# A relative-bias table built in the first stage, with its row copies made from DRAM to DRAM in four pieces on SP's queue

## Chip, core and metric

The kernel runs on one core of one Trainium2 chip. The metric is device time in microseconds; before the change it is 1724.96 us, the median of three runs (1724.55 to 1725.47). The profile is of one further execution.

## What is computed

A transformer of three layers on 512 tokens of width 1024, in float32. The first block is a mixer (a pooling branch beside sparse attention), a cross attention to 256 memory tokens and a SwiGLU network; two hybrid layers of windowed attention and a state space model follow. The change touches the sparse attention alone. Of the reference:

```python
bias = rel_bias_table[_t5_bucket(q_pos[None, :, None] - sel)]
logits = logits + jnp.moveaxis(bias, -1, 1).astype(jnp.float32)
logits = jnp.where(valid[:, None], logits, -jnp.inf)
p = jax.nn.softmax(logits, axis=-1).astype(vg.dtype)
return jnp.einsum('bhtk,btkd->bhtd', p, vg)
```

Each of 8 heads adds to its logits a bias that depends only on the distance from query to key, looked up by bucket in a table of 32 rows. A query attends to the 128 keys with the highest index scores.

## The kernel before

All products are float32 split into two parts: a weight tile of [128, 1024] is loaded raw (`wraw`, three buffers, SP's queue), ScalarE copies its upper part (`whi`, L106), VectorE (DVE) subtracts to get the lower part (`wlo`, L109), and TensorE (PE) runs upper times upper (L148), upper times lower (L149) and lower times upper (L152). A "unit" is 128 output columns: 24 products of 512 tokens.

The order on PE, ScalarE, DVE and Pool (GpSimd) is set by a scheduler when the program is built; each engine then runs its list strictly in order. SP's list stands as the code issues it. A DMA issue that must wait for something holds its engine's queue, and so all that is behind it.

The stages that the change touches are the first (`mem_kv`) and the mixer (`mixer`):

- `mem_kv` multiplies the memory's keys (L646, four units) and values (L671), and meanwhile norms the tokens by halves: squares on ScalarE (L165, L168), sums on DVE (L169), a product with ones on PE that sums over partitions (L175), logarithm, exponential and a Newton step (L188 to L202), then for each of 8 tiles a DVE product (L216), a ScalarE copy (L130) and a DVE subtraction (L131) into the pairs `h`.
- `mixer` first runs three units by token halves, which need `h`. Then come four pool units with window sums and index scores between them, the key and value units, eight query units with the top-128 masks between them (`topk_mask`, DVE, L393 to L407), eight gates (a unit of 24 products, a tanh at L180) each with a product of the pool branch (12 products), and the eight heads. A head is twelve logits products (L523) into two PSUM banks (384 keys of query block 2 in one, 128 and 256 of blocks 0 and 1 in the other, then 512 of block 3 in the first again), a Pool add of bias tile and mask (L528), the softmax on DVE and ScalarE (L415 to L419), transposes (L541), one unit of the other gate between, and the values (L557 to L559).

`bias_tables` stands in the code between the masks and the gates. It loads the table and a one-hot matrix in two halves of 320 columns (L349), multiplies them on PE into a vector of 640 biases by distance for each head (L351, in `pstr`), copies the result to SBUF with DVE (L353, into `G`), and stores it 128 times per head into the DRAM scratch `ts`, [8, 128, 640], from ScalarE's queue (L354). `toeplitz` then loads a head's tile of 128 x 512 from `ts` (L360, ScalarE's queue) with a row step of 639, so that each row is shifted by one column.

Of the kernel before, what the change touches and what calls it, by code (L numbers as in the profile page):

```python
# [13 lines left out]
P = 128  # L14
# [9 lines left out]
# column blocks of the packed per-feature vectors  # L24
# [21 lines left out]
# units of an output projection that run by column halves  # L46
# [3 lines left out]
class Unit:  # L50
    """Weights of an output unit in [128, 512] tiles."""
# [10 lines left out]
class Kern:  # L62
    # [128, 512] four-byte tiles by role; the roles change with the phase
# [14 lines left out]
    # ---------------------------------------------------------------- helpers  # L78
# [20 lines left out]
    def weights(self, src, n=1024):  # L99
        """Load [128, n] raw weights; return them split as hi + lo."""  # L100
        nc = self.nc
        raw = self.wp.tile([P, 1024], F32, tag="wraw", bufs=3, name=self.nm("wraw"))
        nc.sync.dma_start(raw[:, :n], src)
        hi = self.wp.tile([P, 1024], F32R, tag="whi", bufs=3, name=self.nm("whi"))
        lo = self.wp.tile([P, 1024], F32R, tag="wlo", bufs=3, name=self.nm("wlo"))
        nc.scalar.copy(hi[:, :n], raw[:, :n])  # L106
        for o in range(0, n, S):
            c = slice(o, min(o + S, n))
            nc.vector.tensor_tensor(lo[:, c], raw[:, c], hi[:, c].bitcast(F32), ALU.subtract)  # L109
        return hi, lo  # L110

    def held(self, src, tag, n=1024):
        """as weights, in tiles of the activations"""
        nc = self.nc
        raw = self.wp.tile([P, 1024], F32, tag="wraw", bufs=3, name=self.nm("wraw"))
        nc.sync.dma_start(raw[:, :n], src)
        his, los = [], []
        for o in range(0, n, S):
            w = min(S, n - o)
            hi, lo = self.r(tag), self.r(tag)  # L120
            self.split(raw[:, o : o + w], hi[:, :w], lo[:, :w])
            his.append(hi)
            los.append(lo)
        return Unit(his), Unit(los)

    def split(self, src, hi, lo, scale=None):
        """hi + lo = src * scale, both float32r."""
# [13 lines left out]
    def mm3(self, out, w, xs, m=P, start=True, stop=True, woff=0):  # L141
        """out[m, N] += sum_k w_k^T x_k with w = (hi, lo) units and xs = list of (hi, lo)."""
# [28 lines left out]
    def rstd(self, rs, acc, eps, scale=1.0):  # L171
        """acc: per-partition sums of squares; rs = (scale * sum / 1024 + eps)^-0.5 on all partitions."""
        nc = self.nc
        pt = self.ps("tr")[:, : acc.shape[1]]
        nc.tensor.matmul(pt, self.ones, acc, start=True, stop=True)  # L175
        self.inv_sqrt(rs, pt, acc, eps, scale)
# [5 lines left out]
    def inv_sqrt(self, rs, src, u, eps=None, scale=1.0):  # L182
        """u = scale * src + eps, rs = u^-0.5: exp(-ln(u) / 2) and a Newton step; without eps src is u;
        the table with both functions is loaded behind the last square"""
# [19 lines left out]
    def pre_norm(self, gname, h):  # L204
        """returns a function that norms x's columns c into the pairs h"""
# [19 lines left out]
    def pre_scale(self, gname, h, rows=False):  # L225
        """x * g into the pairs h; the norm's token factor, for the products, into the tile returned, a column of it
        per token or, by rows, a row of it per token and a column per block"""
# [22 lines left out]
    def pump(self, n=99):  # L250
        """emit n pieces of the pending tail"""
# [4 lines left out]
    def tail(self, load, mm, use, chain, n, hold=False):  # L256
        """Units 0..7 of an output projection, the last n by column halves: the first half's chain runs under the
        second half's units, the second's under the next phase's first units."""
# [22 lines left out]
    def post_norm(self, gname, eps, otag, src, each, end=None, late=4, pool=(1, 3, 5, 7)):  # L281
        """x + rms_norm(o) * g for x given by src(k, columns): use(j, columns, o) takes o's units, chain(columns)
        has each(k, columns, t) get the sum, end(columns) end a half; DVE adds the squares of the units from late on,
        Pool has the products of the units in pool"""
# [24 lines left out]
    # ---------------------------------------------------------------- constants  # L309
# [32 lines left out]
    def bias_tables(self):  # L342
        """v[h, 511 - dist] = table[bucket(dist), h] in DRAM, a copy per row of the Toeplitz tiles of the T5 bias."""
        nc, a = self.nc, self.a
        tab = self.load("table", [32, 8])
        self.tv = self.dp.tile([8, P, 640], F32, tag="ts", name="ts")
        for c in (0, 320):
# [6 lines left out]
            nc.scalar.dma_start(self.tv[:, :, c : c + 320], v.unsqueeze(1).broadcast_to([8, P, 320]))  # L354

    def toeplitz(self, h):
        """T[p, m] = bias of head h at distance p - m + 384"""
# [5 lines left out]
    # ---------------------------------------------------------------- layer 1: mixer  # L363
# [21 lines left out]
    def topk_mask(self, score):  # L385
        """additive mask: 0 where a key is among the row's first 128, else NEG"""
# [23 lines left out]
    def softmax_rows(self, pt, pr):  # L410
        """pr = softmax(pt + pr) over the rows' columns"""
# [9 lines left out]
    def mixer(self):  # L421
# [4 lines left out]
        # indexer keys and weights  # L426
        # the first units by column halves: the norm of the second runs under them
# [20 lines left out]
        # pool mixer, the index scores in between  # L448
# [13 lines left out]
        for g in range(4):  # L462
# [15 lines left out]
            pooled.append(self.pair(mean, "R"))  # L478
            if g < 3:
# [3 lines left out]
        # shared key and value  # L483
# [15 lines left out]
        self.bias_tables()  # L499
        # gates; the pool branch  # L500
# [10 lines left out]
        # attention, the other gate's projection between the heads  # L511
# [21 lines left out]
        def transposed(prs):  # L533
            """P^T in two parts, for key block kt the query blocks from kt on"""
# [27 lines left out]
        # a head's logits go with the transposes and values of the head before, the other gate's projection in between  # L562
# [13 lines left out]
        # merge  # L576
# [7 lines left out]
        # twice the mixer's output: its norm takes four times the epsilon  # L584
# [12 lines left out]
    # ---------------------------------------------------------------- layer 1: memory  # L597
    def mem_kv(self):
        """keys and values of the memory; the norm's token factor is applied to the products"""
# [39 lines left out]
        for j in range(4):  # L639
# [5 lines left out]
            for k in range(KD):  # L645
                nc.tensor.matmul(pt, wk[j][:, k * P : k * P + P], mg[k], start=k == 0, stop=k == 7)  # L646
        self.h = self.pairs("G")
# [37 lines left out]
    def memory(self):  # L685
        """the tokens' halves one step apart: the first's attention with the second's queries, the second's with the
        first's output projection"""
# [15 lines left out]
        def logits(hd, c):  # L703
            """the probabilities of a half's two query blocks"""
# [81 lines left out]
    # ---------------------------------------------------------------- layer 1: ffn  # L786
    def ffn(self):
# [18 lines left out]
        # the first units by halves  # L806
# [35 lines left out]
    # ---------------------------------------------------------------- layer 2  # L842
# [10 lines left out]
    def hybrid(self, L):  # L853
# [3 lines left out]
        # dt = softplus(dt_raw + dt_bias), a_cs = cumsum(dt * a) within the chunks  # L857
# [3 lines left out]
        # halved convolution weights: conv / 2 feeds silu(x) = (1 + tanh(x / 2)) * (x / 2)  # L861
# [4 lines left out]
        def conv_part(y, j, c, pt, before=None):  # L866
            """y = (conv + bias) / 2 on columns c; before: the products of the columns before c"""
# [22 lines left out]
        # the rows 0..15 of dt's units take the weights' upper parts, the rows 32..47 the lower ones  # L890
# [6 lines left out]
        # the first units by halves  # L897
# [23 lines left out]
        # log1p(e) = ln(u) + (e - (u - 1)) / u with u = 1 + e rounded  # L921
# [15 lines left out]
        # token-major dt and a_cs: [128, chunk, head]  # L937
# [17 lines left out]
        # masked cb^T [s, l] for each group and chunk  # L955
# [10 lines left out]
        # token-major B  # L966
# [16 lines left out]
        def tokens(g):  # L983
            """token-major x * dt of group g, and the states at the chunks' ends"""
# [29 lines left out]
        def decay(j):  # L1014
            """masked cb^T * exp(a_cs[l] - a_cs[s]) of heads 2j, 2j + 1, and exp(a_cs[l])"""
# [17 lines left out]
        def heads(j, ws, ee):  # L1033
            """y of heads 2j, 2j + 1 in place of their xs"""
# [26 lines left out]
        # gate: twice y * silu(z), so the norm takes four times the epsilon  # L1061
# [21 lines left out]
        # sliding window attention: a head's products stack its queries' two parts along the rows, [hi | lo] for  # L1083
        # the even heads and [lo | hi] for the odd ones, and repeat its keys
# [29 lines left out]
        def scores(t, q):  # L1114
            """the probabilities of head t by query block: keys of the block before and its own"""
# [35 lines left out]
        def transposed(prs):  # L1151
            """P^T in two parts: for key block kb the query blocks kb, kb + 1"""
# [16 lines left out]
        def values(j, pts):  # L1169
            """the two heads of a pair share the array, each with half of its columns"""  # L1170
# [17 lines left out]
        # a head's scores go with the transposes of the head before, a unit of products in between  # L1188
# [23 lines left out]
        # out projection, deepnorm residual, layer norm  # L1212
# [80 lines left out]
# ------------------------------------------------------------------ host layout  # L1293
def _units(w):
    """[K, M] -> [M/128, 128, K]: unit u holds for partition p the 128 columns of each K tile."""
# [5 lines left out]
def _rows(w, n):  # L1301
    """[K, M] -> [128, K/128 * M] chunks of n K-tiles each."""
# [33 lines left out]
def layout(inp):  # L1336
# [21 lines left out]
    # attention heads of layer 2, in pairs: an even kv group's head with the next group's  # L1358
# [42 lines left out]
```

## Time and profile before

| | us |
|---|---|
| median of three runs | 1724.96 |
| span of the profiled execution, first to last instruction | 1719.3 |
| PE busy in the span | 1632.6 (95%) |
| DVE busy | 1146.6 (67%) |
| ScalarE busy | 849.0 (49%) |
| Pool busy | 249.6 (15%) |

The profile gives no time of its own for the profiled execution beyond its span; the median stands 5.7 us above the span, which is what lies around the first and last instruction. In the profile a line number names the code line, `out<-in` the tiles by their names, and an idle time is put down to the event that came last before the instruction began. A float32 product on PE that isn't split leaves two records. PE's clock is given as the share granted by the throttle. Waits of an engine other than PE cost time only where PE in turn waits for that engine.

### The profile page before, as it was taken

To read this page: it belongs to the slowest core of one execution; us is meant where nothing else is said; L and a number is where in the kernel's file an instruction comes from. 1 tells how busy PE (TensorE), PEld (TensorE's weight loads), DVE (VectorE), ACT (ScalarE), POOL (GpSimd) and SP (SyncE) were. 2 spreads that over 40 slices of the span, in tenths; PEclk is the share of its full clock that TensorE was granted. 3 is DMA by queue.
4 is the path that set the end of the run, shared out by engine and by line. 5 is a ranking of instruction groups with operands and counts; after the bars stand their busy time and mean duration, and the time that the engine had idled before them with its cause. 6 is when DMAs were issued, how large, how long until landed. Compare 5 with 4: busy or idle time off the path is not lost.

```text
span 1719.3 us, 24715 instructions
## 1 busy us (share of the span) xinstructions
PE 1632.6 (95%) x9078; PEld 1378.1 (80%) x9078; DVE 1146.6 (67%) x2495; ACT 849.0 (49%) x1664; POOL 249.6 (15%) x301
## 2 busy tenths in 40 slices
PE   8999919999898999999999999999999999999996
PEld 6788707888887888888998778787898777888786
DVE  7779517754878555552479876876479986876547
ACT  4532105534566333322366567666256567666424
POOL 2000012201321000000000023122121012312122
PEclk9999959999899999999999999999999999999998
DMA  7322432224224332223562312211253321221133
GB/s 249 126 80 68 101 72 93 72 81 152 87 66 144 98 98 98 93 92 99 149 209 74 121 52 74 74 62 62 91 175 118 114 71 62 74 74 62 62 100 121
DMA packets 59818, 170.70 MB, mean 99 GB/s; under 512 B 6737, under 2 KB 17937, under 8 KB 59697
## 3 DMA queue, kind: packets, MB, share of 16 engines
q1 hardware_dynamic: 49280, 156.79, 28.3%
q10 hardware_dynamic: 10416, 12.34, 3.0%
q8 instruction: 71, 1.16, 0.3%
q14 instruction: 51, 0.41, 0.1%
HBM read 160.18 MB, written 8.91 MB: 98 GB/s over the span
## 4 chain that ended last, share of the span: by engine, by line
PE 79%; DVE 10%; ACT 3%; another core or an unknown queue 3%; DMA 2%; issue 2%; POOL 1%; ACTq 1%; SPq 0%; DVEq 0%; POOLq 0%
PE psmm L152 21%; PE psmm L149 21%; PE psmm L148 21%; DVE wlo L109 2%; PE pstr L1162 1%; PE psmm L1177 1%; PE pstr L1041 1%; DMA wraw<-w_in 1%; PE psmm L646 1%; PE pslg L1133 1%; PE pstr L1047 1%; PE pslg L1134 1%; DVE ht L873 1%; DVE G L299 1%
## 5 line engine op out<-in xcount | busy, mean ns | idle before, releaser
L148 PE MATMUL psmm<-G,whi 128*128 128x512 f32 (+2 forms) x1420 | 525.2, 378 | 3.1 <-ACT whi L106 2.5
L149 PE MATMUL psmm<-G,whi 128*128 128x512 f32 (+2 forms) x1420 | 520.3, 374 | 2.3 <-DVE G L236 2.1
L109 DVE TENSOR_TENSOR wlo<-wraw,whi 128x512 fp32r<-128x512 f32 x541 | 374.4, 713 | 187.5 <-ACT whi L106 166.1
L106 ACT CAST whi<-wraw 128x1024 fp32r<-128x1024 f32 (+3 forms) x275 | 280.9, 1023 | 372.3 <-PE psmm L149 255.8
L152 PE MATMUL psmm<-G,wlo 128*128 128x512 f32 (+2 forms) x1420 | 328.8, 372 | 0.0
L148 PEld LDWEIGHTS psmm<-G,whi 128*128 128x128 f32 (+1 forms) x1420 | 266.7, 189 | 51.0 <-ACT whi L106 4.6
L149 PEld LDWEIGHTS psmm<-G,whi 128*128 128x128 f32 (+1 forms) x1420 | 267.2, 189 | 49.4 <-DVE G L236 3.4
L152 PEld LDWEIGHTS psmm<-G,wlo 128*128 128x128 f32 (+1 forms) x1420 | 251.2, 188 | 46.9 <-issue 1.0
L148 PE MATMUL psmm<-R,whi 128*128 128x256 f32 (+1 forms) x780 | 236.1, 325 | 2.9 <-ACT whi L106 2.3
L149 PE MATMUL psmm<-R,whi 128*128 128x256 f32 (+1 forms) x780 | 236.3, 325 | 1.9 <-DVE R L236 1.9
L148 PEld LDWEIGHTS psmm<-R,whi 128*128 128x128 f32 x780 | 149.1, 191 | 15.3 <-ACT whi L106 2.5
L149 PEld LDWEIGHTS psmm<-R,whi 128*128 128x128 f32 x780 | 149.4, 192 | 14.3 <-DVE R L236 2.7
L152 PE MATMUL psmm<-R,wlo 128*128 128x256 f32 (+1 forms) x780 | 146.9, 327 | 0.0
L152 PEld LDWEIGHTS psmm<-R,wlo 128*128 128x128 f32 x780 | 120.6, 193 | 11.8
L169 POOL TENSOR_TENSOR acc<-acc,sq 128x256 f32<-128x256 f32 (+1 forms) x58 | 61.3, 1061 | 444.4 <-ACT sq L168 439.3
L1143 ACT ACTIVATE w<-w,st 128x256 f32<-128x256 f32 (+1 forms) x128 | 60.1, 471 | 39.0 <-DVE st L1141 38.8
L1148 POOL TENSOR_SCALAR w<-w,st 128x256 f32<-128x256 f32 x64 | 40.5, 643 | 139.9 <-DVE st L1146 122.2
L873 DVE SCALAR_TENSOR_TENSOR ht<-psmm,cwh,ht 128x255 f32<-128x255 f32 (+5 forms) x96 | 57.6, 608 | 2.6 <-ACT ht L871 2.2
L523 PE MATMUL pslg<-G,R 128*128 128x384 f32 (+3 forms) x96 | 20.3, 349 | 40.4 <-DVE st L415 39.9
L528 POOL TENSOR_TENSOR G<-G,G 128x384 f32<-128x384 f32 (+2 forms) x24 | 25.4, 1070 | 211.9 <-DMA G<-ts 160.6
L802 DVE TENSOR_TENSOR sq<-psmm,G 128x512 f32<-128x512 f32 (+1 forms) x24 | 15.5, 646 | 59.0 <-PE psmm L152 58.9
L168 ACT ACTIVATE sq<-G 128x256 f32<-128x256 f32 (+1 forms) x76 | 35.2, 464 | 39.2 <-DVE G L1232 28.3
(322 smaller groups left out, 2331.3 us busy)
## 6 DMA issues: line engine op xcount, KB each, us to landing
wraw<-w_in SPq DMA_DIRECT2D x120, 512.0 KB, 3.4
wraw<-w_out SPq DMA_DIRECT2D x56, 512.0 KB, 3.8
wraw<-w_down SPq DMA_DIRECT2D x24, 512.0 KB, 3.5
wraw<-w_gate SPq DMA_DIRECT2D x22, 512.0 KB, 3.5
wraw<-w_up SPq DMA_DIRECT2D x22, 512.0 KB, 3.4
wraw<-w_down SPq DMA_DIRECT2D x12, 384.0 KB, 3.4
wraw<-w_proj_attn SPq DMA_DIRECT2D x8, 512.0 KB, 3.3
ts<-G ACTq DMA_DIRECT2D x2, 1280.0 KB
```

The lines of the kernel that those rows point to most:

```text
L106: nc.scalar.copy(hi[:, :n], raw[:, :n])
L109: nc.vector.tensor_tensor(lo[:, c], raw[:, c], hi[:, c].bitcast(F32), ALU.subtract)
L148: nc.tensor.matmul(out, whi[:, c], xh, start=start and k == 0, stop=False)
L149: nc.tensor.matmul(out, whi[:, c], xl, start=False, stop=False)
L152: nc.tensor.matmul(out, wlo[:, c], xh, start=False, stop=stop and k == n - 1)
L168: self.last_sq = nc.scalar.activation(t, src, AF.Square)
L169: (eng or nc.gpsimd).tensor_tensor(acc, acc, t, ALU.add)
L523: nc.tensor.matmul(pt, l[:, q], r[:, :N], start=n == 0, stop=n == 2)
L528: nc.gpsimd.tensor_tensor(pr, tb[:, 384 - P * i :], self.cmask if i == 0 else masks[i], ALU.add)
L873: nc.vector.scalar_tensor_tensor(z[:, s:], pt[:, : n - s], cw(3 - s), z[:, s:], ALU.mult, ALU.add)
L1143: nc.scalar.activation(prs[b], prs[b], AF.Exp, bias=nm[:, b : b + 1], accum_out=sm[:, b : b + 1])
L1148: (nc.gpsimd if b % 2 else nc.vector).tensor_scalar(prs[b], prs[b], rc[:, b : b + 1], 1.0, ALU.mult, ALU.mult)
```

## The change

The vector is now made in the first stage: `bias_tables` is called in `mem_kv` between the memory keys' products and the token norm. It stores the vector once, as `t1`, [8, 640], in DRAM. A new function `bias_rows` copies it to 32 of the 128 rows of all heads in `ts`, from DRAM to DRAM, on SP's queue; it is called once behind each of the four pool units.

```diff
@@ bias_tables
         tab = self.load("table", [32, 8])
+        self.v1 = self.dp.tile([8, 640], F32, tag="t1", name="t1")
         self.tv = self.dp.tile([8, P, 640], F32, tag="ts", name="ts")
...
             nc.vector.tensor_copy(v, pt[:8, :320])
-            nc.scalar.dma_start(self.tv[:, :, c : c + 320], v.unsqueeze(1).broadcast_to([8, P, 320]))
+            nc.scalar.dma_start(self.v1[:, c : c + 320], v)
+
+    def bias_rows(self, i):
+
+        rows = slice(32 * i, 32 * i + 32)
+        dst = self.tv[:, rows, :].rearrange("h p c -> p h c")
+        self.nc.sync.dma_start(dst, self.v1[:, :].unsqueeze(0).broadcast_to([32, 8, 640]))
@@ mixer, in the loop over the pool units
             pooled.append(self.pair(mean, "R"))
+            self.bias_rows(g)
             if g < 3:
@@ mixer, between the masks and the gates
-        self.bias_tables()
@@ mem_kv, behind the memory keys
                 nc.tensor.matmul(pt, wk[j][:, k * P : k * P + P], mg[k], start=k == 0, stop=k == 7)
+        self.bias_tables()
         self.h = self.pairs("G")
```

(Comments were blanked as well; from `bias_tables` on, line numbers after the change are 5 to 8 higher.)

The scheduler places the moved work anew. On PE in the first stage, the rows before, where `psmm_185` and `psmm_202` are the third and fourth unit of memory keys and the `pstr` rows are sums of the norms (`acc_227` that of the tokens' first half, `acc_88` that of the memory):

```order
L646 MATMUL psmm_185<-R_162,wraw_118 128x256
L175 MATMUL pstr_251<-acc_227,ones 128x256
L175 MATMUL pstr_292<-acc_88,ones 128x256
L655 MATMUL pstr_302<-ones,acc_88 128x1 x2
L646 MATMUL psmm_202<-R_128,wraw_194 128x256
...
L646 MATMUL psmm_202<-R_162,wraw_194 128x256
L671 MATMUL pslg_313<-wraw_315,R_128 128x512
L671 MATMUL pslg_314<-wraw_315,R_128 128x512
L671 MATMUL pslg_313<-wraw_315,R_132 128x512
L671 MATMUL pslg_314<-wraw_315,R_132 128x512
```

The same place after the change, where the rows with `table` are the two products with the one-hot and `acc_245` is the tokens' sum:

```order
L653 MATMUL psmm_185<-R_162,wraw_118 128x256
L352 MATMUL pstr_217<-G_215,table 8x320
L653 MATMUL psmm_202<-R_128,wraw_194 128x256
...
L653 MATMUL psmm_202<-R_162,wraw_194 128x256
L352 MATMUL pstr_224<-G_222,table 8x320
L175 MATMUL pstr_269<-acc_245,ones 128x256
L679 MATMUL pslg_331<-wraw_333,R_128 128x512
L175 MATMUL pstr_310<-acc_88,ones 128x256
L679 MATMUL pslg_332<-wraw_333,R_128 128x512
L663 MATMUL pstr_320<-ones,acc_88 128x1 x2
```

The sums of the norms moved behind the fourth key unit and both table products. Further down, the sum of the tokens' second half moved from behind the 9th to behind the 14th of the 16 value products.

On SP's queue at the pool units, before (`wraw` rows: the weights of the pool product, of the four pool units and of the key):

```order
L103 DMA wraw_629<-pool_w 128x512
L103 DMA wraw_639<-w_in 128x1024
L103 DMA wraw_714<-w_in 128x1024
L103 DMA wraw_802<-w_in 128x1024
L103 DMA wraw_893<-w_in 128x1024
L103 DMA wraw_957<-w_in 128x1024
```

And after:

```order
L103 DMA wraw_647<-pool_w 128x512
L103 DMA wraw_657<-w_in 128x1024
L361 DMA ts<-t_213 32x8x640
L103 DMA wraw_733<-w_in 128x1024
L361 DMA ts<-t_213 32x8x640
L103 DMA wraw_822<-w_in 128x1024
L361 DMA ts<-t_213 32x8x640
L103 DMA wraw_914<-w_in 128x1024
L361 DMA ts<-t_213 32x8x640
L103 DMA wraw_979<-w_in 128x1024
```

Each row copy stands between the weights of one unit and those of the next.

On ScalarE at the last gates, before (`sq` rows are the tanh of gates, `whi` rows casts of weights, `G<-ts` the loads of the first two heads' bias tiles):

```order
L349 DMA G_1515<-onehot 32x320
L354 DMA ts<-G_1512 1024x1x320
L354 DMA ts<-G_1519 1024x1x320
L180 ACTIVATE sq_1829<-psmm_1804 128x512
L180 ACTIVATE sq_1884<-psmm_1859 128x512
L106 CAST whi_1888<-wraw_1886 128x512
L106 CAST whi_1909<-wraw_1907 128x1024
L106 CAST whi_1943<-wraw_1941 128x512
L360 DMA G_1962<-ts 128x512
L106 CAST whi_2013<-wraw_2011 128x1024
L360 DMA G_2045<-ts 128x512
```

And after, from the tanh of the fifth gate on:

```order
L180 ACTIVATE sq_1779<-psmm_1754 128x512
L367 DMA G_1967<-ts 128x512
L106 CAST whi_1859<-wraw_1857 128x1024
L367 DMA G_2050<-ts 128x512
L106 CAST whi_1893<-wraw_1891 128x512
L180 ACTIVATE sq_1834<-psmm_1809 128x512
L106 CAST whi_1914<-wraw_1912 128x1024
L106 CAST whi_1948<-wraw_1946 128x512
L180 ACTIVATE sq_1889<-psmm_1864 128x512
```

The stores are gone from the queue, and the loads of the bias tiles moved ahead of the casts for the last gates. On PE the first head's first nine logits moved from between the seventh gate and its pool product to behind the last pool product, directly ahead of the other three; from the first head's end on, PE's order is unchanged. Pool's order is unchanged throughout.

## The prediction

> **What bounds the kernel now.** I read the chain of work that ended last first, because it names what the end depends on. Outside one place it is TensorE work. That place, in order of time (start, length, what):
>
> ```profile
> 193.42 8.54 ACTq L354
> 203.15 1.97 ACT whi L106 x3
> 205.12 44.38 another core or an unknown queue
> 249.57 2.60 DMA G<-ts
> ```
>
> The chain goes from the issue of the second table store (L354, on ScalarE's queue) through 44 us in which no engine acts to the load of the first head's bias tile. Next the busy time by stage around it (stretch, length, busy us of PE, PEld, DVE, ACT, POOL, then granted clock, DMA share, GB/s):
>
> ```profile
> 180.00:200.00 20.00, 20.00 (x86) 15.21 (x85) 12.69 (x35) 2.27 (x3) 0.00 (x0) 1.00 0.39 97
> 200.00:216.50 16.50, 14.23 (x58) 11.28 (x57) 3.28 (x5) 3.05 (x5) 0.00 (x0) 0.90 0.59 96
> 216.50:254.00 37.50, 0.07 (x2) 0.05 (x1) 0.67 (x3) 1.04 (x1) 1.70 (x3) 0.53 0.42 76
> 254.00:276.00 22.00, 19.51 (x74) 16.01 (x75) 16.86 (x51) 11.13 (x26) 5.95 (x6) 0.79 0.33 108
> 276.00:296.00 20.00, 19.84 (x110) 16.79 (x109) 14.79 (x52) 10.94 (x28) 7.55 (x8) 1.00 0.26 79
> ```
>
> From 216.5 to 254 all five engines stand still, and on both sides of it the granted clock is 0.90 and 0.79, so some work there runs slowly too. The waits of 185 to 290 us (who waits for whom: total, times, longest) say why:
>
> ```profile
> POOL G L528 <- DMA G<-ts: 160.6, 1, 160.6
> DVE G L415 <- POOL G L528: 47.2, 2, 46.8
> ACT whi L106 <- DMA ts<-G: 44.9, 1, 44.9
> PE pslg L523 <- DVE st L415: 39.9, 2, 37.4
> PE psmm L148 <- ACT whi L106: 2.3, 1, 2.3
> ```
>
> PE waits for the first softmax, DVE there for Pool's bias plus mask, Pool for the bias tile. The tile's load stands on ScalarE's queue waiting for the stores, and a weight cast stands 44.9 us behind it. The queues of 190 to 250 us (packets, MB, share of 16 engines; KB each, us to landing) show the stores themselves:
>
> ```profile
> q10 hardware_dynamic: 2064, 2.62, 36.4%
> ...
> ts<-G ACTq DMA_DIRECT2D x2, 1280.0 KB
> wraw<-w_in SPq DMA_DIRECT2D x3, 512.0 KB, 16.9
> ```
>
> 2.62 MB take from about 192 to 249.6 us, 57.5 us or 14.4 us per 0.66 MB. 36.4% of 16 engines over 60 us is 349 engine-us, 169 ns for each of 2064 packets. The DMA share of 0.42 in the dead stretch is what 6 to 8 of 16 engines would show.
>
> **The gain at the first head.** It is the length of PE's path there less the length that the same work has where nothing disturbs it. Rows of PE's timeline (L152 ends a unit's products; L523 are logits, L541 transposes, L557 values):
>
> ```profile
> 172.06 1.98 PE L152 MATMUL psmm<-G,wlo 128*128 128x512 f32 x8
> ...
> 180.22 1.98 PE L152 MATMUL psmm<-G,wlo 128*128 128x512 f32 x8
> ...
> 189.96 2.11 PE L152 MATMUL psmm<-G,wlo 128*128 128x512 f32 x8
> ...
> 198.25 1.98 PE L152 MATMUL psmm<-G,wlo 128*128 128x512 f32 x8
> ...
> 268.27 1.91 PE L541 MATMUL pstr<-ident,G 128*128 128x128 f32 x8
> ...
> 275.80 0.39 PE L557 MATMUL psmm<-G,G 128*128 128x512 f32 x1
> ...
> 277.65 2.46 PE L523 MATMUL pslg<-G,R 128*128 128x384 f32 x12
> ...
> 284.72 1.97 PE L152 MATMUL psmm<-G,wlo 128*128 128x512 f32 x8
> ...
> 288.38 2.46 PE L523 MATMUL pslg<-G,R 128*128 128x384 f32 x12
> 290.68 1.03 PE L541 MATMUL pstr<-ident,G 128*128 128x128 f32 x8
> ...
> 295.60 1.98 PE L152 MATMUL psmm<-G,wlo 128*128 128x512 f32 x8
> ...
> 306.36 1.98 PE L152 MATMUL psmm<-G,wlo 128*128 128x512 f32 x8
> ```
>
> A gate and its pool product take 172.06 to 180.22, 8.16 us. A head takes 295.60 to 306.36, 10.76 us, its twelve logits 290.68 - 288.38 = 2.30 and its values 277.65 - 275.80 = 1.85. From the unit that ends at 198.25 to the one at 284.72 stand one gate pair (8.16), a pair with the first head's logits (8.16 + 2.30 = 10.46), a head without values (10.76 - 1.85 = 8.91) and a whole head (10.76): 38.3 us undisturbed, against 86.5 measured. The stall is worth 48.2 us: 37.4 + 2.5 + 2.3 of idle PE from the waits above, and 6.0 of slowed clock, which goes with the idleness.
>
> All of it goes if the bias tile is there in time. Its load now stands on ScalarE's queue behind the tanh of the fifth gate, about 65 us earlier. What is late next for Pool is the last mask:
>
> ```profile
> 191.40 0.29 DVE L407 TENSOR_SCALAR G<-G 128x256 f32<-128x256 f32 x1
> ```
>
> At 191.7, with 5 us of adds, it ends near 197; the logits come now after the last pool product, 198.25 + 8.16 + about 4.5 = 211. That covers it by 14 us; Pool's own order does not change. The 512-wide logits now follow the other nine at once and share a bank with the first of them, so a piece of the 2.5 us wait can come back: nothing where later heads run twelve logits in 2.30, 2.5 at most. I take 0.4, near the undisturbed heads.
>
> **The two table products.** 180.22 to 189.96 is 9.74 us, 1.58 over 8.16: that is what the two products with the one-hot cost PE (with their weight loads). They leave this stage, a gain of 1.6, and return in the first stage, where PE is as full: a loss of 1.6, since the weight loads there wait for PE to free buffers. The two copies on DVE and four small issues on ScalarE (0.12 MB in all) move too. The two stores of the vector wait on ScalarE's queue for the copies; behind them stands the norm's logarithm, which needs a PE sum from behind the same products anyway. All this lies beside PE's work, except where it delays the norm:
>
> ```profile
> 20.41 3.70 PE L646 MATMUL psmm<-R,wraw 128*128 128x256 f32 x16
> 23.94 7.89 PE L671 MATMUL pslg<-wraw,R 128*128 128x512 f32 x18
> 31.67 0.59 PE L175 MATMUL pstr<-acc,ones 128*128 128x256 f32 x2
> 37.71 0.68 PE L148 MATMUL psmm<-G,whi 128*68 128x256 f32 x1
> ```
>
> ```profile
> 30.60 0.43 DVE L131 TENSOR_TENSOR G<-ht,G 128x256 fp32r<-128x256 f32 x1
> ...
> 35.68 0.88 DVE L216 SCALAR_TENSOR_TENSOR ht<-G,vecs,rs 128x256 f32<-128x256 f32 x2
> ...
> 50.93 0.42 DVE L131 TENSOR_TENSOR G<-ht,G 128x256 fp32r<-128x256 f32 x1 [0.47 <-ACT G L130]
> ```
>
> PE's sum for the first token half (L175) moves behind the last key unit (3.7) and the products (1.6), 5.3 us. Its last pair was written at 31.0 and used from 37.7, now 39.3: covered. The second half's sum moves from behind 9 value products to behind 14: 5 x 0.88 (7.89 for nine) + 1.6 = 6.0 us, first DVE product at 41.7 instead of 35.7. Up to 51.3 DVE needs only 8 x (0.44 + 0.42) = 6.9 us of 15.7 for these pairs and waits for weights between. So 0 to 6.0 us; I take 0.5, since much of this stretch is waiting.
>
> **The row copies.** Four DMAs of 256 rows of 2560 bytes stand on SP's queue, one behind each pool unit's weights. Behind them wait the weights of pool units two to four and of the key. No trace shows a DRAM to DRAM copy. The nearest rows are the stores' 169 ns per 1280 bytes, and the loads of the whole run:
>
> ```profile
> q1 hardware_dynamic: 49280, 156.79, 28.3%
> ```
>
> 28.3% of 16 engines over 1719.3 us is 158 ns per 3.18 KB, 127 ns for 2560 bytes; the stores' rate gives 338. So 256 packets on 16 engines take 2.0 to 5.4 us per piece, on 8 engines 4.1 to 10.8; the stores as a whole ran 14.4. I take 4, as the new outer loop is 32 rows, not 8 heads. When does a delay reach PE?
>
> ```profile
> 42.47 3.94 SPq L103 DMA_DIRECT2D wraw<-w_in  x2
> ```
>
> ```profile
> 88.00 0.39 PE L148 MATMUL psmm<-G,whi 128*128 128x512 f32 x1
> ```
>
> The first piece goes out at 42.8. With p us per piece, 1.3 per load (128 packets of 158 ns on 16 engines) and 2.6 to land (the bias tile's own row), the key's weights land at 42.8 + 4p + 5.2 + 2.6 = 50.6 + 4p; PE begins that unit at 88.0. The loss is 4p - 37.4, nothing below p = 9.4. Even 10.8 costs 6 us. I take nothing. That cover gone, each us per piece would cost four.
>
> The Trainium skill (DMA: Bandwidth & Descriptors, "Why a DMA increments its semaphore by 16 and not by 1") says that a DMA issued from SP or ACT runs on the largest number up to 16 that divides the slowest dimension of both sides: 8 for the old store, 16 for the new copy. The trace roughly agrees on the first part: 0.42 of 16 engines is 6.7 busy on the mean; by the rule p would lie in 2.0 to 5.4, by the trace alone up to 14.4. The same page ("Issuing engines are not separate DMA queues") speaks against a gain from the move to SP as such.
>
> **Sum.** 48.2 + 1.6 - 1.6 - 0.5 - 0.4 = 47.3 us. The profiled span of 1719.3 becomes 1672.0; the median of 1724.96, 5.7 above the span for what lies around it, becomes 1677.7.
>
> **Rivals.** (a) The second half's norm stays uncovered: all 6.0 instead of 0.5, gain 41.8, 1683.2. For: PE had almost no idle time there. Against: DVE's waits for weights. 0.10. (b) The first head's softmax becomes the next wait. Before, 16 us passed from the landing of the bias tile (252.2) to the transposes (268.3); from logits at 211 to transposes lie 2.3 + 5.4 + 2.3 = 10 us of PE work, so 6 us could show: gain 41.3, 1683.7. Against: Pool's adds are done early now, and later heads show no such wait. 0.06. (c) The change does not spread the copy as its shape says, and the pieces run like the old stores: p = 14.4 costs 20.2 at the key's unit, gain 27.1, 1697.9. For: same bytes, same memory. 0.06. (d) Slower than before: DRAM to DRAM pieces so slow that the pool units starve. It decides from 4p - 37.4 = 47.3, p = 21.2 us; at p = 25 the loss is 62.6 and the time 1740. Against: 21 us is 1.3 us for each of 16 packets per engine, eight times a store's packet. 0.03.
>
> My forecast, gain 44 to 49.8 (the last if no cost returns), has 0.72: 1675 to 1681. The remaining 0.03 lies between it and (c). The range 1675 to 1690 holds forecast, (a), (b) and p up to about 12. A measurement tells 0.2%, 3.4 us, from no change; faster 0.96, same 0.01, slower 0.03.
>
> **What would show it.** Right: no wait of PE over 3 us between 195 and 240 in the new profile, clock 1.00 throughout, Pool's first bias add near 192, pieces that land within 6 us, PE full from 60 to 125. Wrong: a wait of PE for pairs or weights at 38 to 60 (a), at the first transposes (b), for the pool units' or the key's weights (c, d). If the dead stretch is merely shorter, the stores were not what it waited for.

## The result, and the profile after

After the change the kernel takes 1678.3 us (median of 4 runs, 1678.16 to 1680.13), before it 1724.81 (4 runs beside them, 1724.55 to 1725.47). The ratio is 0.9736, 95% interval 0.9724 to 0.9747: 46.5 us less, where 47.3 were forecast, and the time lies 0.6 us from the predicted 1677.7.

The dead stretch is gone. Busy time by stage around the first head, after (start, length, busy us of PE, PEld, DVE, ACT, POOL, then granted clock, DMA share, GB/s):

```profile
180.00:200.00 20.00, 20.00 (x90) 16.57 (x89) 19.06 (x49) 5.60 (x7) 5.64 (x5) 1.00 0.46 150
200.00:216.50 16.50, 16.39 (x77) 13.58 (x76) 7.75 (x18) 6.01 (x10) 2.99 (x4) 1.00 0.38 127
216.50:240.00 23.50, 23.32 (x123) 19.62 (x122) 16.62 (x64) 13.61 (x33) 3.88 (x4) 1.00 0.30 90
```

Where all five engines stood for 37 us, PE is now full and its clock is 1.00 throughout. PE's timeline after, at the ends of the gates (`psmm<-G,wlo`) and the first head's logits:

```profile
184.26 1.98 PE L152 MATMUL psmm<-G,wlo 128*128 128x512 f32 x8
...
192.43 1.98 PE L152 MATMUL psmm<-G,wlo 128*128 128x512 f32 x8
...
200.59 1.98 PE L152 MATMUL psmm<-G,wlo 128*128 128x512 f32 x8
...
208.74 1.98 PE L152 MATMUL psmm<-G,wlo 128*128 128x512 f32 x8
...
213.28 2.45 PE L530 MATMUL pslg<-G,R 128*128 128x384 f32 x12
...
238.85 1.98 PE L152 MATMUL psmm<-G,wlo 128*128 128x512 f32 x8
```

The row at 200.59 is the one that stood at 198.25 before, 238.85 the one that stood at 284.72. Between them lie 38.26 us, where the prediction had worked out 38.3 for undisturbed work and the old trace showed 86.5.

The transfers behind it: ScalarE's queue at the fifth gate, Pool's first bias add, and SP's queue at the pool units (start, time that the queue was held, line):

```profile
186.28 0.33 ACTq L367 DMA_DIRECT2D G<-ts  x1
```

```profile
189.05 1.01 POOL L535 TENSOR_TENSOR G<-G,G 128x384 f32<-128x384 f32 x1 [94.80 <-DMA G<-ts]
```

```profile
45.52 0.70 SPq L361 DMA_DIRECT2D ts<-t  x1
...
47.43 0.83 SPq L361 DMA_DIRECT2D ts<-t  x1
...
56.82 0.54 SPq L361 DMA_DIRECT2D ts<-t  x1
...
60.24 0.54 SPq L361 DMA_DIRECT2D ts<-t  x1
```

The bias tile is loaded at 186.3 instead of 249.6, and the 94.8 us that Pool waited for it cost nothing, since nobody wanted Pool yet. A row copy holds SP's queue for 0.5 to 0.8 us, and the page's list of DMA issues (KB each, median us from issue to landing) has a piece landed in 6.4:

```profile
ts<-t SPq DMA_DIRECT2D x4, 640.0 KB, 6.4
```

Two places lost time. In the first stage, PE's timeline has the two table products (first two rows), and the first index scores (third) start at 64.51 us:

```profile
18.78 0.70 PE L352 MATMUL pstr<-G,table 32*8 32x320 f32 x2
...
23.40 0.70 PE L352 MATMUL pstr<-G,table 32*8 32x320 f32 x2
...
64.51 0.97 PE L381 MATMUL pslg<-R,R 64*128 64x512 f32 x6
```

In the kernel before the same scores start at 62.45, so this stage gave back 2.06 us:

```profile
62.45 0.97 PE L374 MATMUL pslg<-R,R 64*128 64x512 f32 x6
```

The table products make up only part of that: the work behind each begins 0.6 to 0.7 us later, some 1.3 us for both. The largest other piece is a wait that PE did not have before, for the weight cast of one of the mixer's first units (the bracket holds the idle time and what ended it):

```profile
43.79 0.39 PE L148 MATMUL psmm<-G,whi 128*128 128x256 f32 x1 [1.20 <-ACT whi L106]
```

That cast starts on ScalarE at 42.70, before the change at 40.02. In ScalarE's new list it stands behind the steps of the norm of the second token half, which come 6.1 us later than before (its logarithm at 38.84, before at 32.76). A wait of 0.61 us at 19.95 for the memory's norm is gone in return.

At the pool stage PE has another wait that it did not have before, and ScalarE's timeline shows its cause:

```profile
97.72 0.50 PE L148 MATMUL psmm<-R,R 128*128 128x512 f32 x1 [2.10 <-ACT R L130]
```

```profile
90.02 2.00 ACT L106 CAST whi<-wraw 128x1024 fp32r<-128x1024 f32 x2
93.89 1.06 ACT L106 CAST whi<-wraw 128x1024 fp32r<-128x1024 f32 x1 [1.87 <-PE psmm L149]
94.84 0.68 ACT L466 ACTIVATE ht<-psmm,vecs 128x512 f32<-128x512 f32 x1
...
97.04 1.14 ACT L130 CAST R<-ht 128x512 fp32r<-128x512 f32 x2 [0.79 <-DVE ht L484]
```

Three weight casts (L106) stand ahead of the reading of the pool product (L466), and the third waits 1.87 us for PE to free a buffer. The pool product's copy (L130), which PE needs, comes behind all that.

So, up to the third head: 48.2 at the stall, 1.7 at the gates (180.22 to 198.25 before, 18.03; 184.26 to 200.59 after, 16.33), less 4.04 by which the fifth gate's end moved back (180.22 to 184.26: 2.06 and 2.10, to 0.1): 45.9 us. That is 284.72 less 238.85.

### The profile page after: what moved, and what is told of

It reads as the page before. It is cut to its first block, busy times and chain, and to the rows that moved or that the text cites. A ratio compares the mean times of both kernels' runs of the same rounds, so it can differ in the third digit from the quotient of the medians.

```text
span 1678.3 us, 24722 instructions
## 1 busy us (share of the span) xinstructions
PE 1631.3 (97%) x9078; PEld 1380.5 (82%) x9078; DVE 1145.1 (68%) x2495; ACT 850.0 (51%) x1664; POOL 251.8 (15%) x301
## 4 chain that ended last, share of the span: by engine, by line
PE 84%; DVE 9%; ACT 3%; DMA 2%; issue 1%; POOL 1%; DVEq 0%; ACTq 0%; SPq 0%; POOLq 0%
PE psmm L148 23%; PE psmm L149 23%; PE psmm L152 23%; DVE wlo L109 2%; PE pstr L1170 1%; PE psmm L1185 1%; PE pstr L1049 1%; DMA wraw<-w_in 1%; PE pslg L1141 1%; PE pstr L1055 1%; PE psmm L653 1%; PE pslg L1142 1%; PE pslg L1006 1%; PE pslg L1029 1%; DVE G L299 1%
## 5 line engine op out<-in xcount | busy, mean ns | idle before, releaser
L106 ACT CAST whi<-wraw 128x1024 fp32r<-128x1024 f32 (+3 forms) x275 | 281.1, 1024 | 335.0 <-PE psmm L149 262.8
L152 PEld LDWEIGHTS psmm<-G,wlo 128*128 128x128 f32 (+1 forms) x1420 | 251.8, 188 | 46.5 <-issue 1.0
L180 ACT ACTIVATE sq<-ht 128x512 f32<-128x512 f32 (+1 forms) x56 | 31.1, 555 | 47.0 <-DVE ht L802 29.8
L1037 POOL TENSOR_TENSOR R<-R,R 128x512 f32<-128x512 f32 x16 | 20.7, 1291 | 212.7 <-ACT R L1036 212.7
```

Of the source, the lines that this page charges most:

```text
L152: nc.tensor.matmul(out, wlo[:, c], xh, start=False, stop=stop and k == n - 1)
L180: self.nc.scalar.activation(out, src, AF.Tanh, scale=scale)
L1037: (nc.vector if e_ else nc.gpsimd).tensor_tensor(df, df, cb[hd // 8], ALU.mult)
```

## Experiments

Each run has its own ratio to the kernel before on the same chip. The first four shared a chip (before: 1723.21 us, 9 runs), the next three another (1721.69, 7 runs), the last two a third (1723.74, 7 runs).

### The same kernel again

> The changed kernel once more, as the base for the three others of this group. Theory (the stall at the first head is gone for 49.9 us; 2.0 us are lost in the first stage and 2.1 us at the last pool product): about 1678. A second theory, that part of the gain in the medians was chance in the clock: over 1680.

1678.84 us, ratio 0.974 (0.9726 to 0.9753). The scores start at 64.49, and the 2.10 us wait stands at 97.64: both losses come from the program, not from one execution. The first head's logits start at 214.82, though, 1.5 us later than in the other execution: from 80 to 120 us the granted clock is 0.95 and 0.96, where it was 1.00 there. So a position in one trace is good to about 1.5 us only, where the clocks differ.

### The row copies at the queries

```diff
             pooled.append(self.pair(mean, "R"))
-            self.bias_rows(g)
...
             if j in (1, 3, 5):
                 i = 3 - j // 2
                 masks[i] = self.topk_mask(sc[i])
+            if j < 4:
+                self.bias_rows(j)
```

> The four row copies go behind the weights of the first four of the seven later query units instead of the pool units; all else as changed. The theory says that the wait of 2.1 us of PE at the last pool product but one comes from the order of the weight casts on ScalarE, which the copies' place in the code altered: the wait goes and the time is about 2 us below the changed kernel, 1676. The rival, that the copies' traffic itself costs these 2 us wherever it runs: the same time as the changed kernel, within 1 us, and a wait of PE near the copies.

1677.23 us, ratio 0.9731 (0.9718 to 0.9745). PE's wait at that place, and ScalarE's rows before it:

```profile
96.62 0.50 PE L148 MATMUL psmm<-R,R 128*128 128x512 f32 x1 [0.39 <-ACT R L130]
```

```profile
90.83 0.69 ACT L466 ACTIVATE ht<-psmm,vecs 128x512 f32<-128x512 f32 x1
94.46 1.06 ACT L106 CAST whi<-wraw 128x1024 fp32r<-128x1024 f32 x1 [2.94 <-PE psmm L149]
95.95 1.14 ACT L130 CAST R<-ht 128x512 fp32r<-128x512 f32 x2 [0.44 <-DVE ht L484]
```

The reading of the pool product now stands ahead of the casts, and the wait is 0.39 us instead of 2.10. So it was the copies' place in the code that changed the casts' order; by what rule the scheduler does this is not shown. From the first scores (65.15) to the first head's logits (212.17) pass 147.02 us, 148.77 after, both at a clock of 1.00. The scores themselves start 0.6 us later than after, since PE's wait for the last weights of the memory's keys is 1.31 us instead of 0.28. The total is not proven better: the intervals of the ratios overlap.

### The table products at the pool stage

```diff
         wtok = self.s("wtok", (P, 16))
         nc.vector.tensor_copy(wtok, ptw[:, :16])
+        self.bias_tables()
...
-        self.bias_tables()
         self.h = self.pairs("G")
```

with the row copies at the queries as above.

> The table's products also move, from the first stage to the start of the pool stage, and the row copies stay at the query units. The theory (of the 2.0 us lost in the first stage 1.6 are the two products, which cost PE the same in any full stage, and 0.4 the norm's delay): 0 to 1 us below the kernel with the copies at the queries, about 1675.5, and the first stage back at its length before. The rival, that the whole 2.0 us was the norm: 2 us below it, 1674.

1677.56 us, ratio 0.9729 (0.9716 to 0.9742). The first scores start at 62.25, near the 62.45 of before the change, though one of the two products (59.36) now stands ahead of them; the new wait for a cast at 43.8 is gone. So the loss of the first stage comes from the table's place there. But scores to logits take 148.25 (logits at 210.50), 1.2 more than with the table in the first stage: PE is as full here. The median is no lower than with the table in the first stage and the copies at the queries (1677.23), so neither the theory's 0 to 1 us nor the rival's 2 us shows in it.

### No table at all

```diff
         t = self.f("G")
-        sap = self.tv[:, :, :]
+        sap = self.a["w_in"]
...
-            self.bias_rows(g)
...
-        self.bias_tables()
```

The table, the vector and the copies are left out; the bias tiles are loaded from a weight instead, so the biases are not those of the reference.

> Leaves out the table, its vector and the row copies; the bias tiles are loaded from an input weight instead, so the bias is not the reference's. It gives the floor. The theory: 1678.3 less 2.0 and 2.1, about 1674. A rival, that the copies or the table still cost something that no wait shows: under 1672.

1671.14 us, ratio 0.9699 (0.9686 to 0.9712), below the 1672 of the rival and 7.7 us below the changed kernel on the same chip. The first head's logits start at 208.22, 5.1 us earlier than after the change. That is all that the table and the copies still cost ahead of the first head: 2.96 up to the scores (61.55 against 64.51), 2.10 at the pool stage. The other 2 to 3 us of the median lie later, where nothing was left out; no run shows what they are.

### New copies at the old place

```diff
             nc.scalar.dma_start(self.v1[:, c : c + 320], v)
+        for i in range(4):
+            dst = self.tv[:, 32 * i : 32 * i + 32, :].rearrange("h p c -> p h c")
+            nc.scalar.dma_start(dst, self.v1[:, :].unsqueeze(0).broadcast_to([32, 8, 640]))
```

`bias_tables` stands between masks and gates again, as before the change.

> The kernel before with one part of the change alone: the vector is stored once and copied from DRAM to DRAM in the four pieces with 32 rows outermost, but at the old place between masks and gates and on ScalarE's queue. The theory (the old store was slow because it ran on part of the 16 DMA engines; the pieces take 3 to 6 us each): the bias tile comes near 210 to 218 instead of 249.6, PE's dead time shrinks from 37 to under 10 us, the time is 1683 to 1697. The rival, that only the early place pays and the copy is as slow as the store: no change, 1720 to 1728.

1683.51 us, ratio 0.9773 (0.9756 to 0.9791): 38.2 us less than before. ScalarE's queue, where the bias tile's load stood at 249.57 with the old stores:

```profile
194.61 2.61 ACTq L358 DMA_DIRECT2D ts<-t  x4
...
206.51 0.35 ACTq L364 DMA_DIRECT2D G<-ts  x1
206.98 1.05 ACT L106 CAST whi<-wraw 128x1024 fp32r<-128x1024 f32 x1 [5.41 <-DMA ts<-t]
```

The same bytes, on the same queue at the same place, now land within 12 us (194.6 to 206.5) instead of 57. The DMA queues of 194 to 208 us (packets, MB, share of 16 engines) show what is different:

```profile
q10 hardware_dynamic: 1090, 2.62, 60.6%
```

1090 packets in place of 2064 for 2.62 MB. 60.6% of 16 engines over 14 us is 136 engine-us, 125 ns a packet as against 169 for half the bytes. Over the 11.9 us from issue to landing that is 11.4 engines at work for the copies, where the old stores had 349 engine-us in 57.5 us, 6.1 engines; with the weight loads beside them the DMA share is 0.91 from 194 to 208. So of the factor of 4.8 in time, 2.6 is engine time for the same bytes and 1.9 the number of engines. PE keeps short waits for the first softmax, 0.76, 1.11 and 2.69 us, with a clock of 0.89 over 210 to 240.

### The old stores at the new place

```diff
-            nc.scalar.dma_start(self.v1[:, c : c + 320], v)
+            nc.scalar.dma_start(self.tv[:, :, c : c + 320], v.unsqueeze(1).broadcast_to([8, P, 320]))
```

No row copies; `bias_tables` stays in the first stage.

> The kernel before with the other part alone: the table is made in the first stage, but with the old stores of 1.28 MB each from 8 partitions on ScalarE's queue. The theory: the stall at the first head goes (49.9 us), but ScalarE is held some 10 us by the two issues ahead of the norm, and the stores share the DMA engines with the first stage's loads for 57 us: a loss of 8 to 20 us in the first 60 us, 1683 to 1696. The rival, that the place is all that matters: 1676 to 1680.

1712.72 us, ratio 0.9945 (0.9929 to 0.996): only 9 us less than before, far outside both expectations. The first head's logits start at 247.49, and PE has no wait at all between 195 and 275 us, so the early place does end the stall. The time is lost earlier: these logits come 34.2 us later than after the change. ScalarE's timeline (the first row is the two stores' issue on its queue, the second the norm's logarithm behind it) and PE's:

```profile
20.04 30.57 ACTq L354 DMA_DIRECT2D ts<-G  x2
50.66 0.84 ACT L191 ACTIVATE rs<-pstr,eps 128x256 f32<-128x256 f32 x2 [35.02 <-DMA wraw<-w_in]
```

```profile
41.54 9.27 PE L671 MATMUL pslg<-wraw,R 128*128 128x512 f32 x16 [8.98 <-DMA wraw<-w_v_mem]
...
74.91 1.22 PE L175 MATMUL pstr<-acc,ones 128*128 128x256 f32 x2 [23.12 <-DVE acc L169]
```

The issue of two stores holds ScalarE's queue for 30.6 us. The second store's data are in SBUF at 25.2, so at most 5 us of that can be a wait for data. The page's view puts ScalarE's 35.0 us idle down to a weight load, but the row just ahead of it is the issue. The norm's logarithm and the second half's squares stand behind, and PE ends up waiting 23.1 us for the sum of these squares and 9.0 for values' weights, whose loads run beside the stores, 32.1 us together. How much of the loss is the held queue and how much the DMA engines was not taken apart.

### Eight heads as the outer loop of the copy

```diff
-        dst = self.tv[:, rows, :].rearrange("h p c -> p h c")
-        self.nc.sync.dma_start(dst, self.v1[:, :].unsqueeze(0).broadcast_to([32, 8, 640]))
+        self.nc.sync.dma_start(self.tv[:, rows, :], self.v1[:, :].unsqueeze(1).broadcast_to([8, 32, 640]))
```

> As changed, but each row copy has the 8 heads as its outer loop and the 32 rows inside, same bytes and same rows. The theory that the outermost size sets the number of engines (8 instead of 16): the pieces land in 10 to 14 us instead of 6.4, and as the key's weights are late only from 9.4 us per piece, the time is 1678 to 1690. The rival, that the order of the loops does not matter: landing 6.4 us and 1677 to 1680.

1703.01 us, ratio 0.9889 (0.9871 to 0.9906): about 25 us more than after, but not for either reason given. Two parts of the stretch of the loss (columns as above), and PE's waits in it:

```profile
65.00:80.00 15.00, 13.99 (x50) 9.92 (x47) 7.15 (x13) 5.56 (x10) 0.71 (x1) 0.77 0.20 71
...
95.00:110.00 15.00, 9.27 (x27) 7.07 (x27) 6.89 (x15) 4.13 (x7) 1.83 (x3) 0.77 0.10 35
```

```profile
99.99 0.80 PE L148 MATMUL psmm<-G,whi 128*128 128x512 f32 x1 [6.10 <-ACT whi L106]
...
115.73 0.79 PE L148 MATMUL psmm<-G,whi 128*128 128x512 f32 x1 [6.47 <-ACT whi L106]
```

The DMA engines are at 0.10 from 95 to 110, so no copy holds up the weights. PE waits for casts, and ScalarE's rows before the last of these waits show why:

```profile
108.61 0.59 ACT L472 COPY G<-psmm 128x512 f32<-128x512 f32 x1 [8.68 <-PE psmm L152]
109.29 0.69 ACT L465 ACTIVATE ht<-psmm,vecs 128x512 f32<-128x512 f32 x1
113.59 1.14 ACT L130 CAST R<-ht 128x512 fp32r<-128x512 f32 x2 [3.61 <-DVE ht L483]
114.64 2.94 ACT L106 CAST whi<-wraw 128x1024 fp32r<-128x1024 f32 x3
```

ScalarE is idle for 12 us, but in its new list the cast stands behind rows that wait for PE and DVE. From 60 to 125 us PE is idle for 16.0 us, as against 2.5 for the same work after; so about 13.5 of the 25 us are waits, and the rest is slowed clock, 0.79 on the mean. The clock falls first at 68 us, before any wait of more than 0.7 us in that stretch, so what slows it is open. That the scheduler wrote this list because it reckons with slow copies in this form is only argued.

The trace does show how the copies themselves ran. From 64 to 67 us, where the fourth piece moves alone (246 packets, 0.63 MB), the DMA share is 0.52 at 210 GB/s: about 8 of 16 engines, 102 ns a packet. After the change the share reaches 1.00 at 403 GB/s (52 to 54 us). So the theory was right on the number of engines and wrong on the price: at 210 GB/s a piece takes 3.1 us, not 10 to 14, and all four together 12.5 (an estimate from that rate). Eight engines alone do not explain the 57.5 us of the old stores.

### Pieces of 31 rows

```diff
-        rows = slice(32 * i, 32 * i + 32)
-        dst = self.tv[:, rows, :].rearrange("h p c -> p h c")
-        self.nc.sync.dma_start(dst, self.v1[:, :].unsqueeze(0).broadcast_to([32, 8, 640]))
+        for o, n in ((31 * i, 31),) + (((124, 4),) if i == 3 else ()):
+            dst = self.tv[:, o : o + n, :].rearrange("h p c -> p h c")
+            self.nc.sync.dma_start(dst, self.v1[:, :].unsqueeze(0).broadcast_to([n, 8, 640]))
```

> As after, but the four row copies take 31 rows each (the last also the 4 rows left over), so 248 packets of 2560 bytes in place of 256; the order of PE's work stays that of after, ScalarE's in all but a few rows. It tests the formula of the prediction, a loss of 4p - 37.4 us from p = 9.4 us per piece, with a size of p that decides. Theory 1, with the count of DMA engines set by the copy's outer dimension: 31 rows have no divisor up to 16 but 1, one engine moves the piece, 248 packets of about 100 ns are 25 us per piece, and the key's weights land 63 us later than PE wants them: about 1740 us, with waits of PE for the weights of pool units two to four and the key. The Trainium skill (DMA: Bandwidth & Descriptors, the section on the semaphore's 16) states the rule of the largest divisor; no run so far shows it for a copy. Theory 2, the packets spread over the engines whatever the shape: the copies land in 6 to 7 us as after, 1678 us within 2. In between (p = 12, two or more engines): 1689.

1743.11 us, ratio 1.0113 (1.0085 to 1.0141): slower than before the change, by one row less in each piece. The weight casts on ScalarE at the pool units, and PE's rows at the key's unit and the first head:

```profile
76.52 1.04 ACT L106 CAST whi<-wraw 128x1024 fp32r<-128x1024 f32 x1 [17.72 <-DMA wraw<-w_in]
...
102.26 1.04 ACT L106 CAST whi<-wraw 128x1024 fp32r<-128x1024 f32 x1 [12.03 <-DMA wraw<-w_in]
...
127.97 1.04 ACT L106 CAST whi<-wraw 128x1024 fp32r<-128x1024 f32 x1 [18.62 <-DMA wraw<-w_in]
...
154.55 1.04 ACT L106 CAST whi<-wraw 128x1024 fp32r<-128x1024 f32 x1 [8.56 <-DMA wraw<-w_in]
```

```profile
155.65 0.80 PE L148 MATMUL psmm<-G,whi 128*128 128x512 f32 x1 [15.49 <-ACT whi L106]
```

```profile
278.43 2.45 PE L530 MATMUL pslg<-G,R 128*128 128x384 f32 x12
```

Each cast now waits for its weights, and they come 25.7, 25.7 and 26.6 us apart: one piece each, 248 packets in 25.7 us, 104 ns a packet one after the other, where 256 packets of 32 rows land in 6.4 us beside the weights. While a piece moves (76 to 89, 104 to 116, 130 to 142 us) the DMA share is 0.06 to 0.07, one engine of 16. This is the rule of the Trainium skill that the prediction weighed (DMA: Bandwidth & Descriptors, "Why a DMA increments its semaphore by 16 and not by 1"): 31 has no divisor up to 16 but 1. The trace agrees. The prediction's formula gives 4 x 25.7 - 37.4 = 65.4 us for this; the first head's logits moved from 213.28 to 278.43, by 65.2 (63.6 from the other execution of the changed kernel, 214.82).

### The table at the very start

```diff
+        self.bias_tables()          # in consts(), behind the loads of the constants
...
-        self.bias_tables()
         self.h = self.pairs("G")
```

with the row copies at the queries.

> The vector is made at the very start, where PE waits 5 us for its first weights anyway, and the row copies stand behind the first four later query units, where they cost nothing. Theory 1: both losses left in after go, the 2.1 us wait at the pool stage (as with the copies at the queries) and the 2.1 us of the first stage: first index scores at 62 to 63 us instead of 64.5, first head's logits at 209 to 210, 1674 to 1675.5 us. Rival: the loads of the table and one-hots delay the first weights, or the scheduler sets the norm's steps later: no gain over the version with the copies at the queries, 1677 us or more.

1677.14 us, ratio 0.9724 (0.9708 to 0.974), not to be told from after (0.9736, 0.974). The rival's forecast holds, no gain over the version with the copies at the queries. PE's timeline at the start:

```profile
5.37 1.19 PE L655 MATMUL psmm<-R,wraw 128*128 128x256 f32 x2 [5.37 <-DVE R L645]
6.49 1.23 PE L353 MATMUL pstr<-G,table 32*8 32x320 f32 x2
...
17.85 1.13 PE L175 MATMUL pstr<-acc,ones 128*128 128x256 f32 x4 [1.11 <-DVE acc L169]
```

The table products stand behind the 5.4 us wait and not in it, and a wait for the token sum of 1.11 us is new. The scores start at 65.26, the first head's logits at 211.93. No place tried was free: against the kernel without a table (logits at 208.22) the logits come 2.3 us later with the table at the pool stage, 3.7 with it at the very start and 4.0 with it in the first stage, all with the copies at the queries. The two products themselves are 1.3 to 1.8 us of that.

## Why the prediction was right

**The stall** (48.2). Right in mechanism and size: 86.47 us of PE's path became 38.26. With the products that left the gates, 49.9 us were gained here; the prediction had 48.2 + 1.6 - 0.4 = 49.4. The 0.4 for a shared bank did not come: PE has no wait from 195 to 240, and so rival (b), a wait at the first transposes, did not come either.

**What ended it.** The prediction charged the stall to the stores, and left open whether the place or the copy's form mattered, since both take the load off the path. The runs part the two: the form alone gives 38.2 of the 46.5, the place alone only 9, because the old stores, put early, hold ScalarE's queue when the norm needs it, and run on the DMA engines beside the first stage's loads. The place is worth its last 6 us (0.9773 against 0.974 and 0.9736) only together with the form. Within the form, the run with eight heads outermost shows that the number of engines is the smaller part: on 8 engines the copies would take 12.5 us in all. The larger part is how long an engine takes for the same bytes (349 engine-us before, 136 in the copies); whether the longer rows or DRAM as the source shorten it, no run parts.

**The first stage** (-1.6 for the products, -0.5 for the norm). 2.06 measured; that the sum of 2.1 fits is partly luck. The products cost about 1.3. The norm of the second half came 6.1 us later, as worked out (6.0), but reached PE by another way than the one named: not through DVE's pairs, but through a weight cast behind the norm on ScalarE, for which PE waits 1.20 us. Rival (a), the norm uncovered for 6 us, did not come. Three positions of the table gave totals that can't be told apart.

**The row copies** (nothing). This is the step that failed, by 2.1 us. The reason in it held: a piece lands in 6.4 us (the sign named was 6), below the 9.4 from which it would cost; the copies at the old place took 3.0 us each, where 4 was assumed. The formula 4p - 37.4 was right to 2 us where it was put to the test, with p taken from that run. What the step left out is that an added DMA also changes what the scheduler writes for the other engines: three casts went ahead of the reading of a pool product, and PE, forecast "full from 60 to 125", waits 2.10 us at 97.7. The order of ScalarE at the pool units could have been read ahead of time, and was read at the gates only. The run with eight heads outermost shows how large such a thing can get: 13.5 us of waits, and 25 in all with the slowed clock.

**The sum.** 47.3 was forecast, 45.9 shows in the two traces up to the third head, and 46.5 in the medians. The terms missed by 0.5 (stall and gates) and by 2.1 (copies) in opposite ways, so that the total came closer than its worst term is partly luck.

**The slow rivals** (c) and (d) had the mechanism right and needed p over 9.4 and 21.2: 31 rows give p = 25.7 and a kernel slower than before. So the 0.03 was the chance that the shape doesn't spread the copy, and one row decides that.

**The time around the span.** The prediction put 5.7 us around the first and last instruction. The runs show 1.8 (1680.13 with a span of 1678.3). By that the profiled execution of before took about 1721.1 us, 3.5 below the lowest of the four runs; why is not shown. The forecast was made as a difference, so nothing hung on it.

**Where profile and median differ.** The two profiled spans differ by 41.0 us, not 46.5: of the 45.9 gained by the third head, 4.9 are lost again over the rest of the run (4.7 by the last DVE instruction, 1714.24 and 1673.06). The same 130 products of the later attention, before and then after:

```profile
424.00:441.00 17.00, 16.16 (x130) 15.69 (x130) 13.04 (x23) 9.71 (x23) 6.55 (x8) 1.00 0.31 89
```

```profile
378.00:397.00 19.00, 17.89 (x130) 17.42 (x131) 13.50 (x24) 10.21 (x24) 6.57 (x8) 0.91 0.31 84
```

Same instructions, 2.0 us longer, at a granted clock of 0.91 instead of 1.00. The other executions of the changed kernel have spans of 1676.4 to 1676.5, 1.8 us below the profiled one.

## What to carry to other kernels

A table that is copied many times into DRAM should be stored once and spread from there by copies with long rows; that form was worth 38 of 46 us at the old place. Look at the outer dimension of such a copy: with 32 rows outermost it ran on up to 16 engines, with 8 heads on eight, and with 31 rows on one, which turned the gain into a loss. Before a many-row store is moved early, look at which engine issues it and what stands behind: an early place for a slow store ended one stall and made another, of 34 us. And where a scheduler writes the order, read the lists of every engine around each queue that gained an instruction, not only around the place that you want to mend.

## What the runs showed of the hardware that was not expected

- The issue of a DMA can hold its engine's queue for long: two stores of 1.28 MB in 1280-byte rows held ScalarE's 30.6 us in the first stage and 9.9 us at the old place, the copies of the same bytes in 2560-byte rows 2.6. The Trainium skill (DMA: Bandwidth & Descriptors, "Issuing engines are not separate DMA queues") calls the time to initiate a DMA usually small beside the DMA; here it was more than half of the 57.5 us that the two stores took at the old place. At most 5 of the 30.6 us are a wait for data; what the rest consists of stays open.
- A DRAM to DRAM packet of 2560 bytes took 104 ns on one engine (25.7 us for 248) and 102 ns with eight engines at work, less than the 169 ns of a 1280-byte store packet from SBUF.
- The same 130 products ran at a clock of 1.00 in one execution and 0.91 in another, worth 2.0 us in 17. The changed kernel run again had 0.95 and 0.96 from 80 to 120 us, where it had 1.00 the first time. With such slowed stretches about, edits of 1 to 2 us show in the trace but not in the ratios.
